# FFN 2: the differences of x^T's quarters are formed by VectorE from the transposes' PSUM banks, and GpSimd's one is dropped

## The chip, the cores and the metric

One core of a Trainium2 chip runs the whole kernel. Its engines are TensorE (PE, matrix products; PEld is its weight load), VectorE (DVE), ScalarE (ACT), GpSimd (POOL) and SyncE (SP, which here only issues DMAs). The metric is the device time of one execution in microseconds (us), lower is better.

## The reference

One layer of a streaming encoder, on 512 rows of 1024 float32 values:

```
h = x + 0.5 * norm(SwiGLU_1(norm(x)))
u = norm(h)
h = h + norm((sigmoid gates * (recurrent branch, sliding-window attention)) @ w_o)
h = h + 0.5 * norm(SwiGLU_2(norm(h)))        swiglu(x) = (silu(x @ w1) * (x @ w3)) @ w2
```

The norms are RMS norms with a gain. w1 and w3 are 1024 x 2816, w2 is 2816 x 1024. The case is about the step from `@ w_o` and its norm into the products with w1 and w3 of the second SwiGLU (FFN 2).

## The kernel before

Every product is done in three passes: an operand is split into a high part `hi` (rounded to the type fp32r) and the rest `lo = x - hi`, and TensorE adds hi*hi, lo*hi and hi*lo. ACT makes `hi` (line 226), DVE makes `lo` (line 227). So for each weight tile and each activation tile there is an ACT instruction and a DVE instruction before TensorE can start.

*Pair jobs.* The products of FFN 2 with w1 and w3 go two feature tiles (2 x 128) at a time, in a `Pairs` job (lines 985 to 987 are its matmuls). A job multiplies a 2 x 2 arrangement of blocks (weights a11, a12, a21, a22; activations b11, b21, b22 and b12) with seven block products in place of eight, in the manner of Strassen and Winograd. For that it needs sums of weight quarters (S12 and S34) and differences of quarters of x^T, the transposed normalized activations. With x[hh, th] for the half hh of the 1024 features and the half th of the 512 rows these are

```
T[0] = x[0,1] - x[0,0]    T[1] = x[1,1] - T[0]    T[2] = x[1,1] - x[0,1]    T[3] = x[1,0] - T[1]
```

used as t1, t2, t3 and t4. They are split once and serve all 20 pair jobs (10 for w1 and 10 for w3 in turn; this text counts jobs from 0).

*Weight work of a job.* `prep(m, 0)` forms S12 and S34 of job m with four 128x512 instructions on POOL (lines 1038, 1039, 1033, 1034), from two raw tiles loaded by SP (line 150). `prep(m, 1)` to `prep(m, 4)` split raw a, S12, S34 and a22. While TensorE runs job n, the engines prepare splits of job n+1, then POOL sums of job n+2 and loads of job n+3. In a job TensorE uses raw a's part (a11) with b11 first, then S12's first half with t1, then the previous job's a22 with t4, S12's second half with t2, a12 with b21, S34's parts with b22 and t3.

*Work slots.* All these tiles live in 42 slots of 4 KB per partition. A tile takes the slot that has been free longest; if its last reader hasn't finished, the first instruction that writes the tile waits. Each engine works through its own list in program order.

*The step before.* `tok_gemm("wo", ...)` ends the product with w_o. It goes by four row tiles t of 128 rows: `norm(t)` (DVE and ACT), then eight 128x128 transposes on TensorE into two PSUM banks (`transpose_mm`, line 360), then `transpose_out`, where ACT copies hi (line 370) and DVE subtracts lo (line 372) into uT. `transpose_xf` (line 380) copies the same banks in full float32 into xf[half, t // 2] with ACT, because the differences need the unrounded values. For row tiles 2 and 3, this is done at the end, behind `transpose_out(trs[3], 3)`; then `then()` calls `operands()`. Meanwhile TensorE computes the first two feature tiles of w1 and w3 in plain form (accumulators bs[0] to bs[3], lines 237 to 239), and then goes on to job 0.

`operands()` loads ACT's table for Silu (line 1979), forms T[0] and T[1] on DVE (lines 1982, 1984) and splits them (`to_slots`), forms T[2] on POOL (line 1986) and calls `prep(1, 0)`, whose four sums so stand behind T[2] in POOL's list. After `tok_gemm`, DVE forms T[3] (line 1998), the products `silu(bs[0]) * bs[1]` and `silu(bs[2]) * bs[3]` (line 613) are made, T[2] is split between them, `prep(1, 1)` follows, and T[3] is split into uT inside job 0.

Of the kernel before, what the change touches and what calls it, by code (L numbers as in the profile page):

```python
# [13 lines left out]
ALU = mybir.AluOpType  # L14

P = 128
SEQ = 512
D = 1024
# [8 lines left out]
EPS = 1e-6  # L27
# [24 lines left out]
def hybrid_layer(ctx: ExitStack, tc: tile.TileContext, a: dict, out: bass.AP):  # L52
    nc = tc.nc
    act, dve, pool, pe, sp = nc.scalar, nc.vector, nc.gpsimd, nc.tensor, nc.sync
# [8 lines left out]
    def slot(shape, dt=F32, name="s"):  # L63
        uid[0] += 1
        return sb.tile(shape, dt, tag="slot", name=f"{name}_{uid[0]}")

    def bank(name="ps"):
        uid[0] += 1
        return pp.tile([P, 512], F32, tag="ps", name=f"{name}_{uid[0]}")

    def small(w, name="m", bufs=4):
        uid[0] += 1
        return sm.tile([P, w], F32, tag=f"sm{w}", name=f"{name}_{uid[0]}", bufs={1: 11, 4: 12}.get(w, bufs))
# [150 lines left out]
    def split2(hi, lo, src):  # L224

        act.activation(hi, src, AF.Copy)  # L226
        dve.tensor_tensor(out=lo, in0=src, in1=f32(hi), op=ALU.subtract)  # L227
# [15 lines left out]
    def unit(nm, i, **kw):  # L243
        w = get(nm, i)
        ps = bank("f")
        mm_feat(ps, w, **kw)
        return ps
# [116 lines left out]
    def transpose_out(banks, t, xf=None, parts=(0, 1)):  # L364
        c = slice(t * P, (t + 1) * P)
        for half, ps in enumerate(banks):
            ks = slice(half * 4, half * 4 + 4)
            v = ps.rearrange("p (k c) -> p k c", k=4)
            if 0 in parts:
                act.activation(uT[:, 0, ks, c], v, AF.Copy)  # L370
            if 1 in parts:
                dve.tensor_tensor(out=uT[:, 1, ks, c], in0=v, in1=f32(uT[:, 0, ks, c]), op=ALU.subtract)
        if xf:
            transpose_xf(banks, t, xf)

    def transpose_xf(banks, t, xf, halves=(0, 1)):
        for half in halves:
            ps = banks[half]
            v = ps.rearrange("p (k c) -> p k c", k=4)
            act.activation(xf[half, t // 2][:, :, (t % 2) * P : (t % 2 + 1) * P], v, AF.Copy)  # L380


    def tok_gemm(nm, xs, n, R, gpost_name, scale, gpre_name, first, x_to=None, xf=None, spill=False, then=None, eps=D * EPS, pre=None, at_=None, g=None):

# [10 lines left out]
        x_to = x_to or (lambda k: None)  # L397
# [20 lines left out]
        g, us, trs = g or [], {}, {}  # L418
# [122 lines left out]
        t = NT - 1  # L541
# [34 lines left out]
            start(range(1))  # L576
        trs[t] = transpose_mm(us[t])
        transpose_out(trs[t], t)
        transpose_xf(trs[t - 1], t - 1, xf)
        transpose_xf(trs[t], t, xf)  # L580
        if then:
            then()
        if not pre:
# [63 lines left out]
    class Halves:  # L647
# [88 lines left out]
        def operands(self, stage):  # L736

            def xs(m):
                if m not in views:
                    views[m] = slot([P, 2, 2, 256], F32R, name="hx")  # L740
                return views[m]

            def hi(*ms):
                for m in ms:
                    act.activation(xs(m)[:, 0], self.x(0, *self.OPERANDS[m][1:]), AF.Copy)

            def lo(*ms):
                for m in ms:
                    dve.tensor_tensor(out=xs(m)[:, 1], in0=self.x(0, *self.OPERANDS[m][1:]), in1=f32(xs(m)[:, 0]), op=ALU.subtract)

            views = self.views
            if stage == 0:
                hi("m1", "m2")
                self.s1(0)
                lo("m1", "m2")
            elif stage == 1:
                hi("m5")
                self.S((0, 0), (0, 1), (0, 0), 0)
                lo("m5")
            elif stage == 2:  # L760
                hi("m6")
                self.S((0, 1), (1, 1), (0, 0), 0)
                lo("m6")
                self.S((1, 0), (1, 0), (0, 0), 0)
            else:
                hi("m3", "m7", "m4")
                lo("m3", "m7", "m4")
                for u, m in enumerate(self.names):
                    self.ops[u] = *self.parts.pop(u), views.pop(m)
                self.raw.clear()  # L770
                self.hid.eo.clear()
                self.ready = 7
# [563 lines left out]
    ps = [bank("f") for _ in range(NS)]  # L1336
# [6 lines left out]
    for k in range(KT):  # L1343
        if k % 2 == 0:
            split_first(0, k // 2)
        g = vec[:, V_G1 + k : V_G1 + k + 1]
# [126 lines left out]
    def uview(hh, th):  # L1473

        return lambda e, k: uT[:, e, 4 * hh + k, th * 256 : th * 256 + 256]

    def pair_view(p):
        return lambda e, k: p[e][:, k, :]

    def to_slots(src):  # L1480
        p = slot([P, 4, 256], F32R, name="Xh"), slot([P, 4, 256], F32R, name="Xl")
        split2(p[0], p[1], src)
        return pair_view(p)
# [73 lines left out]
    for fn, at_ in zip((gate_kept, silu_kept, swiglu_kept), KEPT_AT):  # L1557
        for f, u in zip(range(NG, NC1), at_):
            half.hooks[u].insert(0, lambda f=f, fn=fn: fn(f))
    xf = {(hh, th): slot([P, 4, 256], name="xf") for hh in range(2) for th in range(2)}  # L1560
    bs = tok_gemm(
        "w2a", hid, FT, len(TAIL_A), "ffn1_post_g", 0.5, "mix_pre_g", [("xr", i) for i in range(4)], xf=xf, spill=True, eps=veps, pre=half,
        at_=(15, 22, 20, X_AT))
# [158 lines left out]
    for i in range(8):  # L1722
        ps = unit("wg", i)
# [16 lines left out]
    for i in range(2):  # L1740
        ps = unit("wk", i)
# [8 lines left out]
    for t in range(NT):  # L1750
        ps = bank("v")
        c = slice(t * P, (t + 1) * P)
        o = ps[:, :256]
# [20 lines left out]
    for i in range(2):  # L1774
        ps = unit("wq", i)
# [135 lines left out]
    for nm, i in att_units:  # L1911
        w = w_first or get(nm, i)
        w_first = None
        ps = bank("f")
# [32 lines left out]
    hid, tn = Hidden(TAIL_B, GS_B), []  # L1947
    X2 = {"b11": uview(0, 0), "b21": uview(1, 0), "b22": uview(1, 1)}
# [3 lines left out]
    gw = []  # L1952
# [9 lines left out]
    for i in range(8):  # L1962
        if i:
            w = get("wao", i, **WAO_AHEAD.get(i, {}))
        ps = bank("f")
# [8 lines left out]
    for at_, fn in zip(MARKS_W, (lambda n: split_to(k_w + len(TS_AT) + n + 1), h_back)):  # L1974
        for n, u in enumerate(at_):
            hooks_w[u].append(lambda n=n, fn=fn: fn(n))
    xf = {(hh, th): slot([P, 4, 256], name="xf") for hh in range(2) for th in range(2)}
    def operands():
        act.activation(small(4, "tiny")[:, 0:1], vec[:, 0:1], AF.Silu)
        t = [slot([P, 4, 256], name="T") for _ in range(4)]  # L1980
        tn.extend(t)
        dve.tensor_tensor(out=t[0], in0=xf[0, 1], in1=xf[0, 0], op=ALU.subtract)
        X2["t1"] = to_slots(t[0])
        dve.tensor_tensor(out=t[1], in0=xf[1, 1], in1=t[0], op=ALU.subtract)
        X2["t2"] = to_slots(t[1])
        pool.tensor_tensor(out=t[2], in0=xf[1, 1], in1=xf[0, 1], op=ALU.subtract)
        pairs_b.prep(1, 0)

    rubbish.append(slot([P, D], name="junk"))
    bs = tok_gemm(  # L1990
        "wo", mixed, KT, len(TAIL_W), "mix_post_g", 1.0, "ffn2_pre_g",
        [("w1b", 0), ("w3b", 0), ("w1b", 1), ("w3b", 1)], xf=xf, spill=True, then=operands, eps=4.0 * D * EPS, pre=half_w,
        at_=(0, 2, 3, XW_AT), g=gw)
    half_w = mixed = hooks_w = None
    rubbish.clear()

# [11 lines left out]
    X2 = pairs_b = None  # L2008
# [58 lines left out]
XW_AT = (1, 2, 3, 4)  # L2067
# [59 lines left out]
```

## Time and profile before

| | us |
|---|---|
| median of 3 runs | 1099.75 (1099.45 to 1100.01) |
| the profiled execution, its own time | 1099.81 |
| its span in the profile | 1098.0 |
| busy in the span: PE, DVE, ACT, POOL | 1087.7, 930.4, 715.4, 405.9 |

The span is the time from the first to the last instruction that the profiler saw; the execution's own time is 1.8 us longer. The granted TensorE clock is 0.999 of full speed. In rows of the timeline stand: start in us, duration in us, engine, line, operation, what it writes and reads, the shape, the count, and in square brackets how long the engine had been idle before it and what ended that. Rows with "x4" merge four instructions that follow one another. In rows of a line or a tile the three numbers are the least, median and greatest duration in ns.

### The profile page before, as it was taken

The numbers are of one execution on the slowest core, as the hardware profiler recorded it, in microseconds if no ns is written. First come the engines' busy times: TensorE is split into PE (matmuls) and PEld (weight loads), VectorE is DVE, ScalarE is ACT, GpSimd is POOL, SyncE is SP. The second block draws the span as 40 slices with busy tenths as digits, with TensorE's granted clock in tenths as the row PEclk, the third lists the DMA queues.
The fourth block names the chain that finished last, engine by engine and source line by source line (L and its number), as shares of the span: only waits on it lengthen the run. The fifth ranks groups of instructions, "written<-read, shape, count | busy, mean of one in ns | idle before, by whom it ended". The sixth has DMA issues, their size and how long they took to land.

```text
span 1098.0 us, 18217 instructions
## 1 busy us (share of the span) xinstructions
PE 1087.7 (99%) x6880; PEld 986.1 (90%) x6880; DVE 930.4 (85%) x1345; ACT 715.4 (65%) x1241; POOL 405.9 (37%) x366
## 2 busy tenths in 40 slices
PE   9999999999999999999999999999999999999997
PEld 7899999998889878899888888888999999998886
DVE  5987999989997998887778866877899989889996
ACT  7756555598767778666656666457555455578872
POOL 0144933232102613242444443111877656633200
PEclk9999999999999999999999999999999999999999
DMA  9325663389866652156222347676423323449923
GB/s 335 126 84 141 126 154 114 105 189 229 235 166 221 155 156 64 39 192 229 66 90 79 120 138 201 170 254 161 147 78 116 105 88 111 145 102 243 211 74 135
DMA packets 56361, 161.72 MB, mean 147 GB/s; under 512 B 5696, under 2 KB 7616, under 8 KB 56272
## 3 DMA queue, kind: packets, MB, share of 16 engines
q1 hardware_dynamic: 39104, 117.77, 31.7%
q0 software_dynamic: 16880, 42.25, 19.7%
q8 instruction: 54, 0.88, 0.3%
q10 hardware_dynamic: 288, 0.52, 0.1%
q14 instruction: 35, 0.29, 0.1%
HBM read 144.81 MB, written 13.62 MB: 144 GB/s over the span
## 4 chain that ended last, share of the span: by engine, by line
PE 96%; DVE 2%; ACT 1%; issue 1%; DVEq 0%; POOL 0%; ACTq 0%; POOLq 0%
PE c L986 13%; PE c L985 13%; PE c L987 13%; PE f L237 9%; PE f L239 9%; PE f L238 9%; PE hw L857 7%; PE hw L856 7%; PE hw L855 7%; PE pt L1850 1%; PE hw L257 1%; PE hw L255 1%; PE hw L256 1%; PE s L1814 1%; PE s L1813 1%
## 5 line engine op out<-in xcount | busy, mean ns | idle before, releaser
L986 PE MATMUL c<-uT,wlo 128*128 128x256 f32 x516 | 146.1, 283 | 1.3 <-DVE wlo L227 1.3
L987 PE MATMUL c<-uT,whi 128*128 128x256 f32 x516 | 146.0, 283 | 0.0
L985 PE MATMUL c<-uT,whi 128*128 128x256 f32 x516 | 146.0, 283 | 0.0
L986 PE MATMUL c<-Xh,wlo 128*128 128x256 f32 x504 | 142.7, 283 | 0.5 <-DVE wlo L227 0.5
L985 PE MATMUL c<-Xh,whi 128*128 128x256 f32 x504 | 142.7, 283 | 0.0
L237 PE MATMUL f<-uT,whi 128*128 128x512 f32 (+1 forms) x392 | 140.7, 359 | 0.1
L238 PE MATMUL f<-uT,wlo 128*128 128x512 f32 (+1 forms) x392 | 139.1, 355 | 0.0
L239 PE MATMUL f<-uT,whi 128*128 128x512 f32 (+1 forms) x392 | 139.0, 355 | 0.0
L987 PE MATMUL c<-Xl,whi 128*128 128x256 f32 x456 | 129.0, 283 | 0.0
L227 DVE TENSOR_TENSOR wlo<-S,whi 128x1024 fp32r<-128x1024 f32 x86 | 122.5, 1426 | 4.1 <-ACT whi L226 2.0
L226 ACT ACTIVATE whi<-S 128x1024 fp32r<-128x1024 f32 x86 | 88.6, 1055 | 30.4 <-DVE S L1034 28.7
L986 PEld LDWEIGHTS c<-uT,wlo 128*128 128x128 f32 x516 | 99.0, 192 | 1.7 <-DVE wlo L227 1.5
L985 PEld LDWEIGHTS c<-uT,whi 128*128 128x128 f32 x516 | 99.0, 192 | 0.2
L987 PEld LDWEIGHTS c<-uT,whi 128*128 128x128 f32 x516 | 99.0, 192 | 0.0
L986 PEld LDWEIGHTS c<-Xh,wlo 128*128 128x128 f32 x504 | 96.7, 192 | 0.7 <-DVE wlo L227 0.7
L985 PEld LDWEIGHTS c<-Xh,whi 128*128 128x128 f32 x504 | 96.8, 192 | 0.3 <-issue 0.3
L857 PE MATMUL hw<-whi,uT 128*128 128x512 f32 x228 | 88.7, 389 | 0.0
L855 PE MATMUL hw<-whi,uT 128*128 128x512 f32 x228 | 88.7, 389 | 0.0
L987 PEld LDWEIGHTS c<-Xl,whi 128*128 128x128 f32 x456 | 87.5, 192 | 0.0
L237 PEld LDWEIGHTS f<-uT,whi 128*128 128x128 f32 x392 | 74.1, 189 | 11.8 <-issue 1.4
L856 PE MATMUL hw<-wlo,uT 128*128 128x512 f32 x216 | 84.0, 389 | 0.0
L239 PEld LDWEIGHTS f<-uT,whi 128*128 128x128 f32 x392 | 74.1, 189 | 10.5
(453 smaller groups left out, 3202.4 us busy)
## 6 DMA issues: line engine op xcount, KB each, us to landing
raw_w3a<-in_w3a_dram SPq DMA_DIRECT2D x21, 512.0 KB, 4.6
raw_w1a<-in_w1a_dram SPq DMA_DIRECT2D x20, 512.0 KB, 4.4
raw_w1b<-in_w1b_dram SPq DMA_DIRECT2D x20, 512.0 KB, 4.2
raw_w3b<-in_w3b_dram SPq DMA_DIRECT2D x20, 512.0 KB, 4.2
raw_w2a<-in_w2a_dram SPq DMA_DIRECT2D x17, 512.0 KB, 6.5
raw_wg<-in_wg_dram SPq DMA_DIRECT2D x16, 512.0 KB, 3.5
raw_w2a<-in_w2a_dram POOLq DMA_DIRECT2D x15, 512.0 KB, 10.4
raw_w2b<-in_w2b_dram SPq DMA_DIRECT2D x15, 512.0 KB, 8.2
```

The source lines that it names most:

```text
L226: act.activation(hi, src, AF.Copy)
L227: dve.tensor_tensor(out=lo, in0=src, in1=f32(hi), op=ALU.subtract)
L237: pe.matmul(ps[:, c0:c1], wh[:, s], h_, start=k == 0 and c0 == 0, stop=False, skip_group_check=True)
L238: pe.matmul(ps[:, c0:c1], wl[:, s], h_, start=False, stop=False, skip_group_check=True)
L239: pe.matmul(ps[:, c0:c1], wh[:, s], l_, start=False, stop=k == KT - 1, skip_group_check=True)
L255: pe.matmul(acc[n], x[:, 0, c], wh[:, s], start=first, stop=False, skip_group_check=skip)
L855: pe.matmul(ps, xs[:, 0, j, c], hi[:, j, :], start=start and j == 0, stop=False, skip_group_check=True)
L856: pe.matmul(ps, xs[:, 0, j, c], lo[:, j, :], start=False, stop=False, skip_group_check=True)
L857: pe.matmul(ps, xs[:, 1, j, c], hi[:, j, :], start=False, stop=i == self.G - 1, skip_group_check=True)
L985: pe.matmul(ps, wh[:, s], xh, start=first, stop=False, skip_group_check=True)
L986: pe.matmul(ps, wl[:, s], xh, start=False, stop=False, skip_group_check=True)
L987: pe.matmul(ps, wh[:, s], xl, start=False, stop=k == 3, skip_group_check=True)
```

## The change

xf keeps only the quarters of the first 256 rows, x[0,0] and x[1,0]. For row tiles 2 and 3 `tok_gemm` calls `differences` instead of `transpose_xf`: DVE takes x[0,1] and x[1,1] straight from the PSUM banks of the transposes and writes T[0] and T[1] in two halves of 128 columns each. T[2] is formed on DVE, as T[1] - x[0,0], which is the same difference. T[3] stays. POOL forms none of them; its list goes from the loads before straight to `prep(1, 0)`.

```diff
@@ tok_gemm(..., g=None, diff=None)
         trs[t] = transpose_mm(us[t])
         transpose_out(trs[t], t)
-        transpose_xf(trs[t - 1], t - 1, xf)
-        transpose_xf(trs[t], t, xf)
+        if diff:
+            diff(t - 1, trs[t - 1])
+            diff(t, trs[t])
+        else:
+            transpose_xf(trs[t - 1], t - 1, xf)
+            transpose_xf(trs[t], t, xf)
         if then:
             then()
@@
-    xf = {(hh, th): slot([P, 4, 256], name="xf") for hh in range(2) for th in range(2)}
+    xf = {(hh, 0): slot([P, 4, 256], name="xf") for hh in range(2)}
+
+    def differences(t, banks):
+        if not tn:
+            tn.extend(slot([P, 4, 256], name="T") for _ in range(2))
+        c = slice((t % 2) * P, (t % 2 + 1) * P)
+        for o, ps, x in zip(tn, banks, (xf[0, 0], tn[0])):
+            dve.tensor_tensor(out=o[:, :, c], in0=ps.rearrange("p (k c) -> p k c", k=4), in1=x[:, :, c], op=ALU.subtract)
+
     def operands():
         act.activation(small(4, "tiny")[:, 0:1], vec[:, 0:1], AF.Silu)
-        t = [slot([P, 4, 256], name="T") for _ in range(4)]
-        tn.extend(t)
-        dve.tensor_tensor(out=t[0], in0=xf[0, 1], in1=xf[0, 0], op=ALU.subtract)
-        X2["t1"] = to_slots(t[0])
-        dve.tensor_tensor(out=t[1], in0=xf[1, 1], in1=t[0], op=ALU.subtract)
-        X2["t2"] = to_slots(t[1])
-        pool.tensor_tensor(out=t[2], in0=xf[1, 1], in1=xf[0, 1], op=ALU.subtract)
+        X2["t1"] = to_slots(tn[0])
+        tn.extend(slot([P, 4, 256], name="T") for _ in range(2))
+        X2["t2"] = to_slots(tn[1])
+        dve.tensor_tensor(out=tn[2], in0=tn[1], in1=xf[0, 0], op=ALU.subtract)
         pairs_b.prep(1, 0)
@@ the call
-        at_=(0, 2, 3, XW_AT), g=gw)
+        at_=(0, 2, 3, XW_AT), g=gw, diff=differences)
```

More of the change, by code (lines that the diff above doesn't have):

```diff
@@ L380, in transpose_xf, with tok_gemm @@
             act.activation(xf[half, t // 2][:, :, (t % 2) * P : (t % 2 + 1) * P], v, AF.Copy)
-    def tok_gemm(nm, xs, n, R, gpost_name, scale, gpre_name, first, x_to=None, xf=None, spill=False, then=None, eps=D * EPS, pre=None, at_=None, g=None):
+    def tok_gemm(nm, xs, n, R, gpost_name, scale, gpre_name, first, x_to=None, xf=None, spill=False, then=None, eps=D * EPS, pre=None, at_=None, g=None, diff=None):
         F = n - R
```

## The prediction

> **What bounds the kernel now.** I read the page's head and chain first, then what TensorE (PE) waited for, then the stretch around the change, engine by engine. First the page's head and engine shares of its chain:
>
> ```profile
> span 1098.0 us, 18217 instructions
> PE 1087.7 (99%) x6880; PEld 986.1 (90%) x6880; DVE 930.4 (85%) x1345; ACT 715.4 (65%) x1241; POOL 405.9 (37%) x366
> PE 96%; DVE 2%; ACT 1%; issue 1%; DVEq 0%; POOL 0%; ACTq 0%; POOLq 0%
> ```
>
> Then all waits of PE in the span (total us, times, longest), and busy time in two stretches (the stretch, its length, PE, PEld, DVE, ACT, POOL, clock, DMA share, GB/s):
>
> ```profile
> PE c L986 <- DVE wlo L227: 1.9, 2, 1.3
> PE w L1305 <- POOL warm L1302: 1.1, 1, 1.1
> PE tr L360 <- DVE hg L350: 0.2, 1, 0.2
> 760.00:782.00 22.00, 21.77 (x183) 21.59 (x182) 15.60 (x23) 16.25 (x32) 10.64 (x6) 1.00 0.54 146
> 782.00:815.00 33.00, 31.13 (x258) 30.72 (x257) 32.76 (x26) 16.48 (x29) 32.37 (x17) 1.00 0.28 95
> ```
>
> PE is the bound. Away from start and tail it waits 0.2 us before the change's place and 1.9 us just behind it. In 782 to 815 us, DVE and POOL are full (32.76 and 32.37 of 33) and PE misses 1.87. The two waits, in PE's timeline:
>
> ```profile
> 812.54 0.39 PE L986 MATMUL c<-uT,wlo 128*128 128x256 f32 x1 [1.34 <-DVE wlo L227]
> 814.77 0.39 PE L986 MATMUL c<-Xh,wlo 128*128 128x256 f32 x1 [0.53 <-DVE wlo L227]
> ```
>
> They stand at the start of pair job 3 (jobs count from 0): its first weight part, then its S12 part, come late from DVE. Without them the two would run at 811.2 and 812.9. So the most that this change can win is about 2.1 us, and what would have to give it is DVE at 812, not at 771 where the edit stands.
>
> **The change part by part.** DVE around it, in order of time (idle time before it in brackets):
>
> ```profile
> 769.56 1.29 DVE L372 TENSOR_TENSOR uT<-tr,uT 128x512 fp32r<-128x512 f32 x2 [0.24 <-ACT uT L370]
> 771.52 1.23 DVE L1982 TENSOR_TENSOR T<-xf,xf 128x1024 f32<-128x1024 f32 x1 [0.67 <-ACT xf L380]
> 774.47 1.62 DVE L227 TENSOR_TENSOR Xl<-T,Xh 128x1024 fp32r<-128x1024 f32 x1 [1.73 <-ACT Xh L226]
> 776.02 2.31 DVE L1984 TENSOR_TENSOR T<-xf,T 128x1024 f32<-128x1024 f32 x1
> 779.45 1.23 DVE L227 TENSOR_TENSOR Xl<-T,Xh 128x1024 fp32r<-128x1024 f32 x1 [1.13 <-ACT Xh L226]
> 782.84 0.68 DVE L613 TENSOR_TENSOR hEO<-f,sw 128x512 f32<-128x512 f32 x1
> 785.67 1.71 DVE L227 TENSOR_TENSOR wlo<-raw_w3b,whi 128x1024 fp32r<-128x1024 f32 x1
> 789.55 2.31 DVE L227 TENSOR_TENSOR wlo<-S,whi 128x1024 fp32r<-128x1024 f32 x1
> ...
> 797.48 2.00 DVE L227 TENSOR_TENSOR wlo<-raw_w1b,whi 128x1024 fp32r<-128x1024 f32 x1 [0.24 <-ACT whi L226]
> 810.51 1.98 DVE L227 TENSOR_TENSOR wlo<-raw_w3b,whi 128x1024 fp32r<-128x1024 f32 x1
> 812.41 2.31 DVE L227 TENSOR_TENSOR wlo<-S,whi 128x1024 fp32r<-128x1024 f32 x1
> 820.01 1.23 DVE L227 TENSOR_TENSOR wlo<-raw_w1b,whi 128x1024 fp32r<-128x1024 f32 x1 [2.12 <-ACT whi L226]
> 830.12 1.21 DVE L227 TENSOR_TENSOR wlo<-raw_w3b,whi 128x1024 fp32r<-128x1024 f32 x1
> ```
>
> ACT and POOL beside it, and SP's loads of job 2 with their time to landing:
>
> ```profile
> 769.90 2.08 ACT L380 ACTIVATE xf<-tr 128x512 f32<-128x512 f32 x4
> 773.40 1.04 ACT L226 ACTIVATE Xh<-T 128x1024 fp32r<-128x1024 f32 x1
> 792.40 0.39 ACT L1083 ACTIVATE ct<-c 128x256 f32<-128x256 f32 x1 [0.54 <-PE c L987]
> 795.28 0.39 ACT L1141 ACTIVATE cc<-c 128x256 f32<-128x256 f32 x1 [1.06 <-PE c L987]
> 796.39 1.05 ACT L226 ACTIVATE whi<-raw_w1b 128x1024 fp32r<-128x1024 f32 x1
> ...
> 772.06 2.96 POOL L1986 TENSOR_TENSOR T<-xf,xf 128x1024 f32<-128x1024 f32 x1 [10.39 <-DMA raw_w3b<-in_w3b_dram]
> 774.99 2.26 POOL L1038 TENSOR_TENSOR S<-raw_w3b 128x512 f32<-128x512 f32 x1
> 784.02 2.28 POOL L1038 TENSOR_TENSOR S<-raw_w1b 128x512 f32<-128x512 f32 x1
> 798.35 2.29 POOL L1034 TENSOR_TENSOR S<-raw_w3b,raw_w3b 128x512 f32<-128x512 f32 x1
> 800.60 2.28 POOL L1038 TENSOR_TENSOR S<-raw_w1b 128x512 f32<-128x512 f32 x1
> 808.23 1.48 POOL L1038 TENSOR_TENSOR S<-raw_w3b 128x512 f32<-128x512 f32 x1
> 821.32 2.29 POOL L1038 TENSOR_TENSOR S<-raw_w1b 128x512 f32<-128x512 f32 x1 [5.45 <-DVE wlo L227]
> ...
> 776.62 2.11 SPq L150 DMA_DIRECT2D raw_w1b<-in_w1b_dram  x2
> DMA to landing us min/median/max: 3.6/3.9/4.4
> ```
>
> A price to note first: the same DVE split costs 1.23 with POOL idle (820.01) and 2.31 with POOL busy (812.41), so one POOL instruction in the way takes 1.08 us.
>
> *ACT.* Four copies go (2.08 us). ACT is far from full here and PE waits for none of it: worth nothing alone. The second pair of transposes' PSUM banks is now freed by DVE, near 773.4, not by ACT at 772.0; PE starts job 0 at 782, so that is covered by some 8 us.
>
> *DVE, first differences.* Two instructions go (1.23 + 2.31 = 3.54). Four halves from PSUM come: the row of that shape, with one operand in PSUM and one strided in SBUF, is L372, 1.29 for two, so 2.58. They begin when L372 ends, 770.85, and end at 773.43. The first T is whole after the third, 772.8; ACT then makes its high part in 1.04, by 773.85, so that split starts 0.6 earlier than 774.47. The idle stretches of 0.67, 1.73 and 1.13 shrink to about 0.4 in all.
>
> *DVE, third difference (from POOL).* Bounds 1.23 and 2.31; I take 2.0, nearer the second since POOL is busy at that time. Removed 3.54, added 2.58 + 2.0: DVE has 1.0 us more work but 3.1 us less idling. From 773.85: four subtractions of 128x1024 (two splits, T[2], T[3]) at 2.0, a product of 0.6, a split at 1.7, a product of 0.6 give 784.8 for the split of raw_w3b that now starts at 785.67. With 1.23 for each wide one it is about 783 (the second product needs PE's fourth accumulator, done at 782); with 2.31 it is 786.6.
>
> *That lead is not kept.* At 797.48 DVE waits for ACT's high part (796.39 to 797.44), which stands behind ACT's L1141, which waited for PE. A DVE that is ahead at 785 stands there until 797.48 all the same. If it were late instead, the next thing late would be job 1's S12 part: it ends at 791.86, PE turns to it at about 792.4, a slack of 0.5. Even at 786.6, 0.9 late, little is left over 0.5.
>
> *POOL.* T[2] goes, 2.96 us. The sums for job 1 stand right behind it; their raw tiles had landed by 772.06 (what ended POOL's wait there), so they start there instead of at 774.99. Next come job 2's sums, now at 784.02: their raws are issued from 776.62 to 778.73 and land up to 4.4 later, at worst 783.1. Slots of the work pool are handed out in the order of their release, and two fewer are held (xf of the second half), so each tile of this time gets a slot released two places sooner, and the second load need not wait for T: issued about 777.0, landed by 781.4. So job 2's sums start 0.9 to 2.9 sooner, I take 2.6, and POOL is done with job 3's sums at 798.0 instead of 800.6. Then it meets a limit that it had not met before 821: there it waited until DVE's split of that job's raw (820.01 + 1.23) released a slot. At job 2 that split starts at 797.48, so job 4's sums start at about 799, 1.6 sooner, and end about 806.7. For job 5's, which start at 808.23 right when PE has passed the part whose slots they take, I assume no earlier start.
>
> *What that does to DVE at 812.* From 797.48 to the end at 812.49 DVE needs 15.0 us for a list which from 820.01 to 831.33 takes 11.3, with POOL then kept waiting at both ends. In the first case some seven POOL instructions stand in the way (that of 798.35, four from 800.60, two from 808.23). After the change the one at 798.35 is done before DVE starts, and small gaps open before 799 and before 808. That is one to two instructions fewer: 1.08 to 2.16 us; I take 1.5. Then the part for 811.2 is ready by 811.0 (the 1.34 go), and S12 by 814.72 - 1.5 = 813.2 against 812.9 (0.3 stays). Gain 1.87 - 0.3 = 1.6. With 1.08 the waits are 0.3 and 0.5, gain 1.1; with 2.16 both go, 1.87.
>
> **Sum.** The profiled execution took 1099.81, 0.06 above the median 1099.75 of the runs shown. 1099.81 - 1.6 = 1098.2. Later jobs start with DVE 2.12 ahead (the idle time at 820.01), so I expect the gain to be carried to the end.
>
> **The rivals.** *No change (1099.3 to 1100.1).* POOL's lead is lost before 797: the loads of job 2 keep their order and POOL again starts near 783 or 784, so the same instructions stand in DVE's way. For it: a lead below about 0.5 us removes no POOL instruction from DVE's list. Against it: slots come two places sooner.
>
> *Slower (1100.7 to 1102.3).* The four PSUM differences lose to POOL as wide ones do: 0.65 + 1.08 each, 6.9 us in all, ending at 777.8. The list of wide ones then runs without a gap, 8.0 + 0.6 + 1.7 + 0.6, to 788.7, and job 1's S12 part, 3.9 behind (as 789.55 behind 785.67) and 2.31 long, is done at 794.9 against 792.4: PE waits 2.5 there. Everything behind shifts with it, so of the old 1.87 between 0.3 and all of it comes on top: 2.5 + 0.3 - 1.87 = 0.9 to 2.5 us more than now. It decides as soon as that part is over 0.5 + 1.6 = 2.1 us late, slack and gain together. Against it are rows of instructions with a PSUM operand:
>
> ```profile
> L1106 DVE TENSOR_TENSOR cc<-c,ct x20: 409/411/418, 791.8 to 986.5; 128x256 f32<-128x256 f32 x20
> L1118 DVE TENSOR_TENSOR cc<-ct x20: 411/1512/1522, 794.0 to 984.0; 128x256 f32<-128x256 f32 x20
> ```
>
> L1106 (one operand in PSUM) takes 0.41 in all 20 jobs, with POOL busy or not; L1118 (both in SBUF) goes from 0.41 to 1.51. L613 at 782.84, from PSUM too, took 0.68 amid busy POOL. The Trainium skill, "SBUF — State Buffer", section "SBUF: two separate sides", says that a VectorE instruction with two SBUF inputs and a GpSimd instruction take the shared port pair as an exclusive lock, the loser blocking for the whole instruction. By that rule the new differences, with one SBUF input, stay at 0.65 and the rival falls; T[2], with two, now competes with POOL, which the bound 2.31 holds. The trace agrees in these two rows; a 128x512 difference from PSUM into SBUF at this very place is not in it.
>
> *The order of slots.* All later tiles get other slots, so some load or sum may wait for a later release, or one fewer. Every wait after 815 is hidden now; a surprise is of the order of the waits above, 1 to 3 us either way.
>
> **How the numbers follow.** Gain of 1.1 to 1.9: 0.60 (1097.9 to 1098.7). No change: 0.18. Slower by the PSUM reads: 0.08. Slots: 0.14, on both sides. The range, 1097.3 to 1100.4, holds the first two, with some scatter, and the milder part of the others. 0.2% is 2.2 us, about what a measurement of this kernel tells from no change; the main case lies just inside. Faster by more: 0.06 of the main case by scatter and 0.06 of the slots, 0.12. Slower by more: 0.05 of the PSUM reads and 0.05 of the slots, 0.10. The rest, 0.78, is within.
>
> **What the profile after would show.** L380 x4 at 770 gone, four 128x512 subtractions of about 0.65 on DVE from 770.9; POOL's first sum at about 772 and its first waits before 800; the split of raw_w1b still at about 797.5, waiting for ACT; that of raw_w3b done by 811.2; PE's waits on L227 at 0.3 instead of 1.9. I am wrong if PE waits near 792, if the subtractions take over 1 us, or if POOL still runs without a gap from 775 to 815.

## The result, and the profile after

| | before | changed |
|---|---|---|
| median, us (12 runs each) | 1099.68 (1099.21 to 1100.68) | 1097.12 (1096.84 to 1097.87) |
| ratio (95% interval) | | 0.9978 (0.9970 to 0.9985) |
| the profiled execution's own time | 1099.81 | 1097.87 |
| its span | 1098.0 | 1096.1 |

The kernel became 2.6 us faster, and the whole interval of the ratio lies below 1. 1.6 was forecast, and 1097.12 lies 0.2 below the range. The profiled execution of the changed kernel is the slowest of its twelve. Lines of the code behind the edit have moved: 985 to 987 are now 989 to 991, 1033 to 1039 are 1037 to 1043, 1083 is 1087.

The head of the page after, all waits of PE (total us, times, longest), and the two stretches of before (columns as there):

```profile
span 1096.1 us, 18214 instructions
PE 1087.6 (99%) x6880; PEld 986.5 (90%) x6880; DVE 928.4 (85%) x1348; ACT 713.1 (65%) x1237; POOL 399.3 (36%) x365
...
PE w L1309 <- POOL warm L1306: 1.1, 1, 1.1
PE tr L360 <- DVE hg L350: 0.3, 1, 0.3
...
760.00:782.00 22.00, 21.71 (x183) 21.54 (x182) 18.42 (x27) 13.73 (x27) 8.74 (x6) 1.00 0.55 164
782.00:815.00 33.00, 33.00 (x277) 33.00 (x276) 31.43 (x28) 17.76 (x31) 28.93 (x16) 1.00 0.32 111
```

PE's wait of 1.9 us on L227 is gone and 782 to 815 is full: 33.00 where 31.13 stood. POOL fell from 32.37 to 28.93 there, DVE from 32.76 to 31.43. DVE and POOL, then SP's loads of job 2 and, behind the second mark, PE's first use of S12's low part in job 3, selected rows, all after (this profile runs 0.24 later than that of before when it comes to 768):

```profile
771.01 0.68 DVE L1988 TENSOR_TENSOR T<-tr,xf 128x512 f32<-128x512 f32 x1
773.04 0.69 DVE L1988 TENSOR_TENSOR T<-tr,T 128x512 f32<-128x512 f32 x1
778.35 2.31 DVE L1995 TENSOR_TENSOR T<-T,xf 128x1024 f32<-128x1024 f32 x1
784.57 1.72 DVE L227 TENSOR_TENSOR wlo<-raw_w3b,whi 128x1024 fp32r<-128x1024 f32 x1
797.71 1.22 DVE L227 TENSOR_TENSOR wlo<-raw_w1b,whi 128x1024 fp32r<-128x1024 f32 x1 [1.57 <-ACT whi L226]
798.93 1.22 DVE L227 TENSOR_TENSOR wlo<-S,whi 128x1024 fp32r<-128x1024 f32 x1
806.88 0.68 DVE L227 TENSOR_TENSOR w<-raw_w1b,w 128x512 fp32r<-128x512 f32 x1
807.82 1.21 DVE L227 TENSOR_TENSOR wlo<-raw_w3b,whi 128x1024 fp32r<-128x1024 f32 x1
808.95 2.31 DVE L227 TENSOR_TENSOR wlo<-S,whi 128x1024 fp32r<-128x1024 f32 x1
...
772.44 1.29 POOL L1042 TENSOR_TENSOR S<-raw_w3b 128x512 f32<-128x512 f32 x1 [10.54 <-issue]
781.09 1.87 POOL L1042 TENSOR_TENSOR S<-raw_w1b 128x512 f32<-128x512 f32 x1 [1.51 <-DMA raw_w1b<-in_w1b_dram]
799.01 2.29 POOL L1042 TENSOR_TENSOR S<-raw_w1b 128x512 f32<-128x512 f32 x1 [1.71 <-DVE wlo L227]
808.40 1.77 POOL L1042 TENSOR_TENSOR S<-raw_w3b 128x512 f32<-128x512 f32 x1 [1.73 <-PE c L990]
776.22 0.82 SPq L150 DMA_DIRECT2D raw_w1b<-in_w1b_dram  x2
...
812.72 0.28 PE L990 MATMUL c<-Xh,wlo 128*128 128x256 f32 x1
```

POOL starts at 772.4, waits for job 2's loads until 781.09, and waits twice more where it had run without a gap: 1.71 before job 4's sums and 1.73 before job 5's. In or beside those two gaps DVE's splits of raw_w1b, S12, a22 and raw_w3b take 1.22, 1.22, 0.68 and 1.21, where before they took 2.00, 2.31, 1.78 and 1.98. The two of those rows of before that are not shown further up:

```profile
799.41 2.31 DVE L227 TENSOR_TENSOR wlo<-S,whi 128x1024 fp32r<-128x1024 f32 x1
808.48 1.78 DVE L227 TENSOR_TENSOR w<-raw_w1b,w 128x512 fp32r<-128x512 f32 x1
```

Job 3's S12 part is done at 811.26, 13.55 after the start at 797.71; before it was 17.24 (797.48 to 814.72).

What that is worth to PE can be read without its wait rows, from the ACT copy that follows the first block product of a job. Job 1 and job 4, before and then after:

```profile
792.40 0.39 ACT L1083 ACTIVATE ct<-c 128x256 f32<-128x256 f32 x1 [0.54 <-PE c L987]
825.02 0.38 ACT L1083 ACTIVATE ct<-c 128x256 f32<-128x256 f32 x1 [0.54 <-PE c L987]
...
792.64 0.38 ACT L1087 ACTIVATE ct<-c 128x256 f32<-128x256 f32 x1 [0.54 <-PE c L991]
822.88 0.38 ACT L1087 ACTIVATE ct<-c 128x256 f32<-128x256 f32 x1 [0.54 <-PE c L991]
```

Three jobs took 32.62 before and take 30.24 now. 30.24 is what PE needs alone: 3 jobs of 84 matmuls, one each 0.12 us in an unbroken row. So 2.38 us came out of these three jobs, and there is no more in them.

### The profile page after: what moved, and what is told of

Same layout as the page of the kernel before. It is cut to its first block, busy times and chain, and to the rows that moved or that the text cites. A ratio compares the mean times of both kernels' runs of the same rounds, so it can differ in the third digit from the quotient of the medians.

```text
span 1096.1 us, 18214 instructions
## 1 busy us (share of the span) xinstructions
PE 1087.6 (99%) x6880; PEld 986.5 (90%) x6880; DVE 928.4 (85%) x1348; ACT 713.1 (65%) x1237; POOL 399.3 (36%) x365
## 4 chain that ended last, share of the span: by engine, by line
PE 95%; DVE 2%; ACT 1%; issue 1%; DMA 0%; DVEq 0%; SPq 0%; ACTq 0%
PE c L990 12%; PE c L989 12%; PE c L991 12%; PE f L237 9%; PE f L238 9%; PE f L239 9%; PE hw L861 7%; PE hw L860 7%; PE hw L859 7%; PE pt L1854 1%; PE hw L257 1%; PE hw L256 1%; PE hw L255 1%; PE s L1818 1%; PE s L1817 1%
## 5 line engine op out<-in xcount | busy, mean ns | idle before, releaser
L227 DVE TENSOR_TENSOR wlo<-S,whi 128x1024 fp32r<-128x1024 f32 x86 | 121.4, 1413 | 4.1 <-ACT whi L226 2.0
```

## The experiments

Theory: what decides is how far POOL's sums are when VectorE comes to its list at 797; POOL's lead opens gaps in its work, in which VectorE's wide splits run at their own speed. Rivals: VectorE's shorter idling and ScalarE's lighter load near 771; or only that POOL has one instruction less. Each was timed beside the kernel before (medians 1099.80 and 1099.74 in the two sets). Below, "job 1's mark" is the first of the two ACT rows shown last (792.40 before, 792.64 after), and "three jobs" is the time from it to the second, in each kernel's own profile.

**T[2] on VectorE alone.** On the kernel before:

```diff
-        pool.tensor_tensor(out=t[2], in0=xf[1, 1], in1=xf[0, 1], op=ALU.subtract)
+        dve.tensor_tensor(out=t[2], in0=xf[1, 1], in1=xf[0, 1], op=ALU.subtract)
```

> The kernel before with one word changed: T[2] = x[1,1] - x[0,1] is formed by VectorE at its old place; ScalarE's copies of xf and the SBUF-to-SBUF T[0] and T[1] stay. Theory (POOL's lead decides, and the differences from PSUM are what pays for T[2] on VectorE): POOL starts job 1's sums near 772 as in the changed kernel, so PE's two waits at job 3 shrink or go; but VectorE, with 2.3 us more work and its old idle stretches, brings job 1's S12 part near 794.5 against 792.4, a new PE wait of about 2 us there. Time 1099 to 1100, no gain. Rival (the relief of POOL alone is the whole gain): no wait near 792, 1097.1 to 1097.5.

Measured: 1098.16 us, ratio 0.9986 (0.9977 to 0.9995), three jobs 30.70. The wait near 792 did not come, and most of the gain was there; the time lies between the two ranges that had been expected. VectorE and POOL of this kernel:

```profile
781.68 1.22 DVE L1986 TENSOR_TENSOR T<-xf,xf 128x1024 f32<-128x1024 f32 x1
786.80 1.71 DVE L227 TENSOR_TENSOR wlo<-raw_w3b,whi 128x1024 fp32r<-128x1024 f32 x1
...
783.77 1.43 POOL L1038 TENSOR_TENSOR S<-raw_w1b 128x512 f32<-128x512 f32 x1 [3.19 <-DMA raw_w1b<-in_w1b_dram]
800.68 2.22 POOL L1038 TENSOR_TENSOR S<-raw_w1b 128x512 f32<-128x512 f32 x1 [1.16 <-DVE wlo L227]
```

T[2] cost VectorE 1.22, not 2.3: it fell into the 3.19 us that POOL stood waiting for loads. VectorE is 0.3 later at the split of raw_w3b than before (786.80, in a profile that is 0.84 later at job 1's mark; 785.67 before), and the time falls all the same. The expectation's rival was nearer than its theory; the differences from PSUM aren't needed to pay for T[2]. This one word gives 1.9 of the 2.4 us that the whole change takes out of the three jobs.

**The differences from PSUM alone.** On the changed kernel:

```diff
-        dve.tensor_tensor(out=tn[2], in0=tn[1], in1=xf[0, 0], op=ALU.subtract)
+        pool.tensor_tensor(out=tn[2], in0=tn[1], in1=xf[0, 0], op=ALU.subtract)
```

> The changed kernel with T[2] = T[1] - x[0,0] formed by POOL, in front of job 1's sums: the differences from PSUM alone. Theory (POOL's lead decides): T[2] can start on POOL only when T[1] is whole, near 773.7, so the sums for job 1 start near 776.7, later than in either kernel; VectorE's list from 797.5 again meets two to three POOL instructions more, and PE's waits at job 3 return with 1.5 to 3 us: 1098.7 to 1100.5. Rival (VectorE's shorter idling and ScalarE's relief decide): VectorE is further ahead at 785 than in the changed kernel, and the time stays at 1096.8 to 1097.4.

Measured: 1099.95, ratio 1.0003 (0.9994 to 1.0012), three jobs 32.76. As the theory says:

```profile
784.44 1.72 DVE L227 TENSOR_TENSOR wlo<-raw_w3b,whi 128x1024 fp32r<-128x1024 f32 x1
797.46 2.17 DVE L227 TENSOR_TENSOR wlo<-raw_w1b,whi 128x1024 fp32r<-128x1024 f32 x1 [1.45 <-ACT whi L226]
...
785.04 2.27 POOL L1042 TENSOR_TENSOR S<-raw_w1b 128x512 f32<-128x512 f32 x1
800.75 2.28 POOL L1042 TENSOR_TENSOR S<-raw_w1b 128x512 f32<-128x512 f32 x1
...
PE c L990 <- DVE wlo L227: 2.0, 2, 1.5
```

VectorE is 1.2 us ahead at 784, waits 1.45 for ScalarE at 797 and has nothing left of it. POOL, without a gap, is where it was before, and so is PE's wait. ScalarE is relieved of its copies here too, so its lighter load alone gives no gain either.

**POOL held back by work that nobody reads.** On the changed kernel, in front of job 1's sums, n = 2 and then n = 1:

```diff
+        for _ in range(n):
+            pool.tensor_tensor(out=rubbish[0].rearrange("p (k c) -> p k c", k=KT), in0=f32(uT[:, 0, :, 384:512]), in1=f32(uT[:, 1, :, 384:512]), op=ALU.subtract)
         pairs_b.prep(1, 0)
```

> The changed kernel with two 128x1024 subtractions put in front of job 1's sums on POOL; they write a scrap tile that nobody reads, so VectorE, ScalarE and slots are as in the changed kernel. They start near 771.2 and take 2.4 to 3.0 us each, so the sums for job 1 start near 776.5 instead of 772.4. Theory (POOL's lead decides): PE's two waits at job 3 return in full or more, 2 to 4 us with the restarts: 1099 to 1101. Rival (VectorE's and ScalarE's relief near 771 decides): no more than 0.3 us is lost, 1096.8 to 1097.5.

> The changed kernel with one scrap 128x1024 subtraction put in front of job 1's sums on POOL; it starts near 770.9 and takes about 2.4, so job 1's sums start near 773.4 instead of 772.4. In the changed kernel POOL waited 1.51 for the loads of job 2. Theory (what counts is when job 2's sums start, and so POOL's place at 797): the 1 us is taken from that wait, job 2's sums start at 781.1 to 782, and no PE wait of over 0.1 returns: the changed kernel's time within 0.3. Rival (each us that POOL is later costs its share at 812): 0.5 to 1 us slower than the changed kernel.

Measured: with two 1100.47, ratio 1.0007 (0.9999 to 1.0016), three jobs 33.32, PE's waits on L227 2.3 us; with one 1097.42, ratio 0.9978 (0.9970 to 0.9987), three jobs 30.24, no such wait. POOL with two, then with one:

```profile
770.92 4.90 POOL L1997 TENSOR_TENSOR junk<-uT 128x1024 f32<-128x1024 f32 x2 [9.27 <-DVE uT L372]
775.79 2.27 POOL L1042 TENSOR_TENSOR S<-raw_w3b 128x512 f32<-128x512 f32 x1
801.31 2.28 POOL L1042 TENSOR_TENSOR S<-raw_w1b 128x512 f32<-128x512 f32 x1
...
772.65 2.41 POOL L1997 TENSOR_TENSOR junk<-uT 128x1024 f32<-128x1024 f32 x1 [9.27 <-DVE uT L372]
800.76 2.21 POOL L1042 TENSOR_TENSOR S<-raw_w1b 128x512 f32<-128x512 f32 x1 [1.16 <-DVE wlo L227]
```

(The last profile is 1.7 us later at job 1's mark, so 800.76 there is 799.0 beside the others.) Two idle instructions take the whole gain away with everything else of the change in place: this is the test that speaks most directly for POOL's place. One costs nothing that these runs can tell: its time came mostly out of POOL's wait for job 2's loads (those sums start at 782.98, counted from job 1's mark only 0.4 later than in the changed kernel), and both later gaps are still there. As an aside, the four differences from PSUM ran at 0.68 or 0.69 each while the two idle instructions kept POOL busy: they don't lose to it.

**Two slots held.** On the changed kernel:

```diff
         if not tn:
+            held.extend(slot([P, 4, 256], name="held") for _ in range(2))
+            for x in held:
+                act.activation(x[:, 0, 0:1], vec[:, 0:1], AF.Copy)
             tn.extend(slot([P, 4, 256], name="T") for _ in range(2))
...
+        for x in held:
+            dve.tensor_copy(small(4, "tiny")[:, 0:1], x[:, 0, 0:1])
+        held.clear()
         pairs_b.prep(1, 0)
```

> The changed kernel with two more work slots held from the differences to the end of operands, as many as before (two tiny writes by ScalarE and two tiny reads by VectorE hold them). By the order of slots the second load of job 2 then waits for T[2] on VectorE, near 780.7, and lands near 784.6, so job 2's sums start there and not at 781.1, though job 1's still start at 772.4. Theory (POOL's lead at 797 decides, and the freed slots give a good part of it): PE's waits at job 3 return with 1 to 2.4 us, 1098.2 to 1099.6. Rival (it is enough that POOL has one instruction less): 1096.9 to 1097.5.

Measured: 1098.30, ratio 0.9987 (0.9979 to 0.9996), three jobs 30.74. Loads and sums moved as expected, but PE's wait came back with only 0.3, where 1 to 2.4 had been expected:

```profile
776.70 4.23 SPq L150 DMA_DIRECT2D raw_w1b<-in_w1b_dram  x2
784.50 1.91 POOL L1042 TENSOR_TENSOR S<-raw_w1b 128x512 f32<-128x512 f32 x1 [5.05 <-DMA raw_w1b<-in_w1b_dram]
793.10 1.47 POOL L1042 TENSOR_TENSOR S<-raw_w3b 128x512 f32<-128x512 f32 x1
799.90 2.28 POOL L1042 TENSOR_TENSOR S<-raw_w1b 128x512 f32<-128x512 f32 x1
808.24 1.35 POOL L1042 TENSOR_TENSOR S<-raw_w3b 128x512 f32<-128x512 f32 x1 [0.69 <-PE c L990]
...
PE c L990 <- DVE wlo L227: 0.3, 1, 0.3
```

Job 2's sums start 0.5 later than before (784.50 against 784.02), yet job 4's start 0.7 earlier (799.90 against 800.60): VectorE, ahead, stood idle for 2.43 in front of 797.55, and three of POOL's four sums of job 3 took 1.3 to 1.6, where before two did and two took 2.3. The same three are short with PSUM alone, where VectorE stood for 1.45. So a lead of VectorE need not be wholly lost: POOL can take it up. The median, 1098.30, is in the range that the theory gave, but the three jobs kept 1.9 of their 2.4 us: most of the gain needs only that POOL has the one instruction less, and the two freed slots bring 0.5.

All kernels side by side. Job 4's sums are counted from job 1's mark in the same profile; the gap is POOL's wait before job 5's sums; VectorE's list runs from the start of the split of raw_w1b near 797 to the end of job 3's S12 part. The last column is the median less that of the kernel before in the same set.

| kernel | job 4's sums start | POOL's gap before job 5's | VectorE's list | three jobs | median |
|---|---|---|---|---|---|
| two idle POOL instructions | 8.9 | 0 | 17.5 | 33.32 | +0.67 |
| PSUM alone, T[2] on POOL | 8.4 | 0 | 17.4 | 32.76 | +0.15 |
| before | 8.2 | 0 | 17.2 | 32.62 | 0 |
| T[2] on VectorE alone | 7.4 | 0.73 | 15.3 | 30.70 | -1.64 |
| two slots held | 7.4 | 0.69 | 15.4 | 30.74 | -1.50 |
| one idle POOL instruction | 6.6 | 1.53 | 13.7 | 30.24 | -2.32 |
| changed | 6.4 | 1.73 | 13.6 | 30.24 | -2.56 |

The order is the same in all columns of the profiles, but for the two kernels at 7.4, which are alike within 0.05 there; the medians follow the three jobs within 0.4. It isn't an even slope. VectorE's list falls by 1.9 us between 8.2 and 7.4 and by 1.6 us between 7.4 and 6.6; PE gains 1.9 us by the first step and only 0.5 by the second, because little of its wait was left. Job 5's sums start when PE frees their slots, near 808.2. A POOL that reaches that point just in time (before) has no gap; one that is 0.7 early has one, and there the a22 split of VectorE takes 0.68 instead of 1.78.

**The changed kernel again, and two kernels beyond it.** The second divides the additions of job 15 for the product with w2, and the third also gives PE more to do before the last transposes:

```diff
-            late[end - 4, 1] = [lambda i=i: half.s1(i) for i in range(4)]
-            late[end - 3, 1] = [lambda: half.load(3)]
+            late[end - 4, 1] = [lambda i=i: half.s1(i) for i in range(2)]
+            late[end - 3, 1] = [lambda: half.load(3)] + [lambda i=i: half.s1(i) for i in (2, 3)]
...
-            start(k0)
+            start(range(5))
         else:
...
-            mm_feat(bs[3], ws[3], 0, 256, ks=k1)
+            mm_feat(bs[3], ws[3], 0, 256, ks=range(5, KT))
```

> The changed kernel once more, for a comparison on one chip. Theory: 2.0 to 2.6 us below the kernel before; between the start of FFN 2's first products and job 4 its TensorE runs 2.38 us less than before (1.87 of the waits as listed and 0.5 that the two restarts cost), and near 942 a wait of 0.3 to 0.4 may stand. Rival (the pair of profiles overstates it): 1.6 to 1.9 us below.

> The changed kernel with the four 128x512 additions that job 15 makes for the product with w2 (6.9 us on VectorE in one stretch) divided: two in job 15, two in job 16. Theory: the split of job 16's raw_w1b, done at 942.56 in the changed kernel just after PE wanted it, comes 3.4 us sooner; the PE wait of 0.3 near 942 (0.4 with its restart) goes and none comes in job 16 or 17, where VectorE had idle time of 1.1 and 2.9: 0.2 to 0.5 us below the changed kernel. Rival (the wait moves on to the next job's split): the same time.

> The kernel with the divided additions, and with five instead of four feature tiles of the fourth product placed in front of the last row tile's transposes (in both calls of tok_gemm that take this path), so that PE has 0.36 us more to do while it waits 0.29 for VectorE's hg near 768. Theory: that wait goes, uT's last part comes under 0.1 later and is not what anything waits for: 0.2 to 0.4 us below the kernel with the divided additions. Rival (the listed wait is only the transposes' own start-up): the same time.

Measured, on the chip that also ran the one idle instruction: changed again 1096.96, ratio 0.9974 (0.9964 to 0.9984); divided additions 1097.25, 0.9976 (0.9967 to 0.9986); with the fill 1096.79, 0.9973 (0.9962 to 0.9983). The first profile of the changed kernel had a PE wait in job 16:

```profile
942.20 0.28 PE L989 MATMUL c<-uT,whi 128*128 128x256 f32 x1
942.61 0.39 PE L990 MATMUL c<-uT,wlo 128*128 128x256 f32 x1
942.84 0.28 PE L991 MATMUL c<-uT,whi 128*128 128x256 f32 x1
```

Matmuls in a row start every 0.12, here 0.41 and 0.23 apart: 0.4 us lost, where the split of raw_w1b came just late behind the additions. In the second profile of the same kernel only 0.1 is lost there, so the wait is on the edge and differs between executions. With the additions divided it doesn't appear, and no difference in time can be told. With the fill, the wait of 0.3 before the transposes is missing from PE's waits, but it is missing too in the profile with the divided additions alone, so that the fill took it away isn't shown. The median with the fill is the lowest of all, but the intervals of the three lie over each other: a faster kernel than the changed one is not shown. In all three profiles the three jobs take 30.24 and job 4's sums start 6.4 behind job 1's mark, as in the first profile of the changed kernel.

## Why the prediction was right or wrong

*The bound, and where the time lies: right.* The time came out of PE's two waits at job 3.

*First differences: right.* Four ran at 0.68 or 0.69, first at 771.01, last done at 773.73 (with the shift of 0.24, 773.5 against 773.43 forecast). T[2] took 2.31, the upper bound; 2.0 was taken. The split of raw_w3b started at 784.57, 0.2 from the 784.8 forecast.

*"That lead is not kept": right here, too narrow as a rule.* VectorE waited for ScalarE until 797.71, as said, and POOL's sums of job 3 took as long as before (7.7 us). With two slots held POOL's sums of that time were faster, which the step left out.

*POOL: right.* Forecast 772 for the first sums, 2.6 us of lead for job 2's, about 799 for job 4's after a wait for VectorE's split: 772.44, 781.09, 799.01. For job 2's second load the forecast was an issue near 777.0 and landing by 781.4: SP issued the two from 776.22 to 777.04, and the sums that need them started at 781.09.

*VectorE at 812: the first of two terms that were too small.* "One to two instructions fewer: 1.08 to 2.16 us; I take 1.5." It was 3.7 (17.24 to 13.55). The prediction had this number in its own lines: 15.0 us for the list up to the split of raw_w3b at 797, 11.3 for the same list at 820, where POOL was kept waiting at both ends. After the change that list takes 11.3 (797.71 to 809.03). The prediction put two gaps in POOL's work at about one of VectorE's instructions each. Each gap let two splits through: those of raw_w1b and S12 at 797.71 and 798.93, those of a22 and raw_w3b at 806.88 and 807.82. So instead of 0.3 of the second wait staying, VectorE was some 1.5 us ahead of PE at job 3's S12 (done at 811.26, used at 812.72). Since only the 0.3 was left to win there, this mistake of 2.2 us in the list is worth 0.3 us in the time.

*The price of PE's waits: the second term that was too small.* The prediction took the listed 1.87 as all that could be won there. Around the two waits, before:

```profile
812.54 0.39 PE L986 MATMUL c<-uT,wlo 128*128 128x256 f32 x1 [1.34 <-DVE wlo L227]
812.76 0.28 PE L987 MATMUL c<-uT,whi 128*128 128x256 f32 x1
812.88 0.28 PE L985 MATMUL c<-uT,whi 128*128 128x256 f32 x1
813.96 0.28 PE L985 MATMUL c<-Xh,whi 128*128 128x256 f32 x1
814.77 0.39 PE L986 MATMUL c<-Xh,wlo 128*128 128x256 f32 x1 [0.53 <-DVE wlo L227]
814.99 0.28 PE L987 MATMUL c<-Xl,whi 128*128 128x256 f32 x1
```

The second wait is listed with 0.53. But the starts are 0.81 and then 0.22 apart where unbroken ones are 0.12 apart: 0.79 lost. So this wait costs its idle time and some 0.26 more. In the rows, unbroken matmuls of 0.28 each start 0.12 apart and so lie over one another, while the first after a wait is shown with 0.39 and the next starts only 0.22 later; what in the engine makes it so, the rows don't show. Two such, and 1.87 becomes 2.38, as the three jobs say. For the same reason PE would have come to the two places unbroken at 811.0 and 812.5, not at 811.2 and 812.9. With 2.38 for the term, 1099.81 - 2.38 = 1097.4 would have been the forecast. Of the 1.0 us between the gain forecast and that measured, the first term makes 0.3 and this one 0.5.

*The rivals.* Slower by the PSUM reads: the reads took what the trace of before said. No change: POOL's lead did come. The order of slots: its part is the earlier load of job 2, worth 0.5 us in the three jobs (30.74 to 30.24).

*What stays open.* The medians differ by 2.56 and, in the second set, by 2.78; the three jobs explain 2.38. With T[2] on VectorE alone and with two slots held the medians gain 0.3 to 0.4 less than the three jobs say. Single profiles differ by up to 1.7 us at job 1's mark, so such a rest of 0.2 to 0.4 can't be placed, nor told from the measurement's own uncertainty (0.9970 to 0.9985 is 1.6 to 3.3 us). That the gaps in POOL's work let the splits run at 1.22 is shown by rows that coincide; a kernel in which POOL's sums are taken away from 797 to 812 alone was not run.

## What to carry to other kernels

An instruction removed from one engine can pay 40 us later on another: follow its queue forward to the place where the bound engine waits, and ask there what the removal opens. Price the waits of a pipelined engine by the distance of starts before and behind them, not by the listed idle time alone. Look for a stretch of the same work without the disturbance: it had the right time for the list. Where two engines slow each other, count gaps: most of the gain came in one step when the one engine began to wait for its slots, a further lead of 1 us was worth 0.5, and one more idle instruction then changed nothing.

## What was not expected of the hardware

While VectorE and POOL both run instructions with two operands in SBUF, each takes nearly the sum of the two: 128x1024 on VectorE 2.31 and 128x512 on POOL about 2.2, against 1.22 with POOL waiting and 1.3 beside VectorE's differences from PSUM (772.44). The prediction counted only VectorE's side of it (1.08). POOL's side is as large, and it fits that POOL is faster where VectorE stands idle: the same eight sums took 16.6 us before (784.02 to 800.60) and 15.4 with two slots held (784.50 to 799.90).
